# One more pair of head jobs as sums of blocks, leaner head chunks and five attention units at once, in a hybrid mLSTM and windowed-attention step

## The chip, the core and the metric

One core of a Trainium2 chip runs the whole program in one launch. The metric is device microseconds from start to end. Before the change the median of three runs is 858.66 us (856.5 to 862.46).

## The reference

One layer of a hybrid decoder, on a prompt of 1024 tokens and on 8 decoding samples of 4 tokens each (together 1056 columns), model width 1024:

```
h = rmsnorm(x, g) * (1 + scale(c)) + shift(c);  gate(c)          # c: condition vectors
mq, mk, mv, mi, mf, mo, mz, aq, ak, av, az, gm, ga = split(h @ w_in)
# mLSTM branch: 4 heads of 128, chunks of 128 tokens; per chunk
s   = (q k^T) * exp(dmat - m_hat);  num = s v + w_inter * (q C)
dot = sum(s) + w_inter * (q n);     y = num / max(|dot|, exp(-m_hat))
C'  = decay * C + (w_end * k)^T v;  n' = decay * n + sum(w_end * k)
# attention branch: 8 query heads, 2 key heads of 64, window 128, sinks
o = softmax(q k^T, sink) v
x + gate * ((sigmoid(gm) * (y_m @ w_mo) + sigmoid(ga) * (y_a @ w_ao)) @ w_o), then a final rmsnorm
```

Results are y for prompt and samples, the mLSTM states C, n, m, and the kept keys and values.

## The kernel before

Everything is transposed: tiles have channels on the 128 partitions and tokens along the free side. A large product is done in three parts, for accuracy near float32: operands are split into a high and a low part (`split4`, `block_split`: ACT rounds the high part, DVE subtracts), and hi*hi, hi*lo and lo*hi are added up in one PSUM bank.

**Jobs.** A job is one 128-channel slice of `h @ w_in`: `job` loads and splits its weights one or two jobs ahead (`prefetch`, `preload`, in the list `order`) and calls `piece` three times, for 384, 384 and 288 columns. Each piece is 24 products (8 row blocks of h times three parts). `keep` in `head_jobs` moves the result out of PSUM and stores it in the DRAM tiles `mD[h]` (q, k, v of a head).

**Summed pairs.** `block_products` does two jobs at once with a scheme of seven block products in place of eight: the 1024 prompt columns and the 1024 rows of h are cut in halves, and seven sums or differences of blocks (`t1` to `t4` and plain blocks of h, in `OPERANDS`) are multiplied by sums and differences of weight blocks. Each of the seven is 12 products of 512 columns, so a pair has 84. The sample columns go in 16 small products (`Pair.samples`, `smp`) and one more (`smpo`). PSUM banks are carried from product to product, `filled` copies a bank that two products build on. `sum_blocks` forms `t2`, `t3`, `t4` and then `t1` from h read back from DRAM (`hD`, tiles `hb`); `hook` lets pair 0 wait, in the order written out, for `t2` at its product 6 and `t1` at its product 5. `Pair(head_kv, 3)` makes k and v of head 3; 8 pairs of gates, 2 of query gates and 4 of head gates follow.

**Side work.** TensorE's order is written out by the program (`in_order`): the large products come in sequence, and after each group of three `side.tick()` may put in a step of other work. `Side` keeps streams, each with a largest number of live items and a shortest time between beginnings, in a planned time `side.now` that products move on. A step ends in a `yield` of a lag and of the PSUM banks ("b", "o", "a") that its next step needs; steps that need banks come no sooner than `quiet` after the last visit. Streams: "m" gate values and `head(h)`; "a" attention `unit(g, b0)` (16 of them: scores, softmax, transposes `pt`, products `oT`); "x" `ada_gate`, `sum_blocks` and loads; "s" `sample_attention` and `sample_head(h)`. `side.finish` runs what is left of a stream at once; `side.until` lets planned time pass. DVE and ACT get their order from the scheduler of the language in the part after the first stage, and SP issues all transfers in order.

**A head.** `head(h)` goes over its 8 chunks in groups of 3, 3 and 2 (`GROUPS`): `load` fetches q, k, v and two broadcast rows; `stage_a` turns k (`tk`, into `kn`) and v (`tv`, into `vn`) and scales vn by `wend` into `vw`; `stage_a1` and `stage_a2` form the decay matrix `et` with DVE and the exponential; `stage_b` makes `S`, multiplies, and carries the state C on by `U`; `stage_c` to `stage_d` form the result, its norm and its transpose. A group holds seven half tiles: q, k, v, et, qw, kn, vn. All such tiles come from one pool of 43 (`ht`).

**After the pairs** come 16 jobs with `w_ao` and `w_mo`, then the output product `fo` with the residual and the last norm.

Of the kernel before, what the change touches and what calls it, by code (L numbers as in the profile page):

```python
# [10 lines left out]
F32 = mybir.dt.float32  # L11
# [161 lines left out]
def body(tc, a):  # L173
    nc = tc.nc
    with ExitStack() as ctx:
# [76 lines left out]
        side = Side(stores, {"m": (2, 35.0), "a": (4, 9.0), "x": (2, 0.0), "s": (1, 0.0)}, 2.0)  # L252
# [626 lines left out]
        def sample_attention():  # L879
            qpad, vns, kTs = at["qpad"], at["vns"], at["kTs"]  # L880
            kc, vc, kcT = ([ht([128, 4, 128], f"{n}{u}") for u in range(2)] for n in ("kc", "vc", "kcT"))
# [8 lines left out]
            for u in range(2):  # L890
                tq = pb([128, 4, 128], f"kctp{u}")
                for j in range(4):
                    tr(tq[:, j], kc[u][:, j], ident)
                S.copy(kcT[u], tq)
                yield 3.0, "b" if u == 0 else "o"
            sc = po([128, 2, WIN + NS], "scs")
            for u in range(2):
                for w in range(4):
                    b = u * 4 + w
                    qb = qpad[:, b].rearrange("p k g t -> p (k g t)")  # L900
                    r = slice(32 * w, 32 * w + 32)
                    mm(sc[r, u, 0:WIN], qb, kcT[u][:, w], start=True, stop=True)
                    mm(sc[r, u, WIN:], qb, kTs, start=True, stop=True)
# [21 lines left out]
            pT = ht([128, 4, 128], "pTs")  # L925
# [41 lines left out]
        def head_jobs(h):  # L967
            mD[h] = [dp.tile([128, SEQ], F32, name=f"{n}D{h}") for n in "qkv"]
# [28 lines left out]
        mD = {}  # L997

        def head(h):
# [15 lines left out]

            def stage_a(p):
                cs = GROUPS[p]
                m, j0 = len(cs), h * 8 + cs[0]
                w = m * 128
                q, k, v, e_, qw = w_[p]  # L1020
                t129 = lambda t: t[:, :387].rearrange("p (c e) -> p c e", e=129)
                tk = pb([128, 3, 128], f"tk{h}_{p}")
                for i, c in enumerate(cs):
                    tr(tk[:, i], k[:, i * 128:i * 128 + 128], ident)
# [3 lines left out]
                for i, c in enumerate(cs):  # L1028
                    tr(tv[:, i], v[:, i * 128:i * 128 + 128], ident)
# [6 lines left out]
                et, ns = e_[:, :384].rearrange("p (c e) -> p c e", e=128), t129(e_)  # L1036
                w_[p] = q, k, kn, vn, vw, et, qw, ns

            def stage_a1(p):
                m = len(GROUPS[p])  # L1040
                q, et, qw = w_[p][0], w_[p][5], w_[p][6]
                V.tensor_tensor(et[:, :m], et[:, :m], cmask.unsqueeze(1).to_broadcast((128, m, 128)), op=ALU.add)
                V.tensor_tensor(qw[:, :m], qw[:, :m], q[:, :m * 128].rearrange("p (c e) -> p c e", e=128), op=ALU.mult)

            def stage_a2(p):
                j0 = h * 8 + GROUPS[p][0]
                et = w_[p][5]
                for i in range(len(GROUPS[p])):
                    S.activation(et[:, i], et[:, i], AF.Exp, bias=an[:, j0 + i:j0 + i + 1])

            def stage_b(p):
                cs = GROUPS[p]
                m, j0 = len(cs), h * 8 + cs[0]
                q, k, kn, vn, vw, et, qw, ns = w_[p]
                S_ = po([128, 3, 128], f"S{h}_{p}")
                for i, c in enumerate(cs):
                    mm(S_[:, i], k[:, i * 128:i * 128 + 128], q[:, i * 128:i * 128 + 128], start=True, stop=True)
                V.tensor_tensor(et[:, :m], et[:, :m], S_[:, :m], op=ALU.mult)
# [12 lines left out]
                w_[p] = vn, et, qw, chain, ns  # L1071
# [41 lines left out]
            for visit in ([(load, 0), 10.0, "b"], [(stage_a, 0), 3.0, ""], [(stage_a1, 0), 4.0, ""], [(stage_a2, 0), 6.0, "o"],  # L1113
                          [(stage_b, 0), (load, 1), 10.0, "ob"], [(stage_c, 0), (stage_a, 1), 3.0, ""], [(stage_c2, 0), (stage_a1, 1), 4.0, ""],
                          [(stage_a2, 1), 6.0, "o"], [(stage_b, 1), (stage_c3, 0), (load, 2), 4.0, "b"], [(stage_d, 0), 6.0, "ob"],
                          [(stage_c, 1), (stage_a, 2), 3.0, ""], [(stage_c2, 1), (stage_a1, 2), 4.0, ""], [(stage_a2, 2), 6.0, "o"],
                          [(stage_b, 2), (stage_c3, 1), 4.0, "b"], [(stage_d, 1), 6.0, "o"], [(stage_c, 2), 3.0, ""], [(stage_c2, 2), 7.0, ""], [(stage_c3, 2), 5.0, "b"],
                          [(stage_d, 2), 0.0, ""]):
                for fn, p in visit[:-2]:
                    fn(p)  # L1120
                yield visit[-2:]
# [264 lines left out]
        class head_kv:  # L1386
            names = lambda h: (("mk", h), ("mv", h))
            ahead = lambda self, i: None

            def evac(self, c, th, *src):  # L1390
                t = ht([128, 512], "mkv")
                if len(src) == 2:
                    V.tensor_tensor(t, src[0], src[1], op=ALU.add)
                else:
                    S.copy(t, src[0])
                store(mD[self.i][1 + c][:, HALF[th]], t)
                self.held[c, th] = True
                if len(self.held) == 4:
                    side.add("m", head(self.i))

            def samples(self, o):
                for c, t in enumerate((ks, vs)):
                    V.tensor_copy(t[:, self.i], o[:, c])
# [136 lines left out]
        order += [(n, h) for h in range(NH) for n in ("mq", "mk", "mv") if h < NH - 1 or n == "mq"]  # L1540
# [151 lines left out]
        pairs = [Pair(head_kv, NH - 1)] + [Pair(gate, d) for d in range(KT)] + [Pair(query_gate, i) for i in range(2)] + [Pair(head_gate, h) for h in range(NH)]  # L1692

        def hook(n, i):
            if n == 0 and i in (6, 5):
                side.until(lambda: {6: "t2", 5: "t1"}[i] in formed)
            if i == 6:
                if pairs[n].kind is query_gate:
                    side.until(lambda: len(units_done) == 16)
                side.until(lambda: len(samples_done) >= {head_kv: 0, gate: 0, query_gate: 1, head_gate: pairs[n].i + 2}[pairs[n].kind])  # L1700
# [226 lines left out]
```

## Time and profile before

| | before |
|---|---|
| median of 3 runs | 858.66 us |
| profiled execution: time / span of its instructions | 857.83 us / 856.0 us |
| mean granted TensorE clock | 0.995 |
| TensorE busy | 832.8 us |
| DVE busy | 564.8 us |
| ACT busy | 387.6 us |
| GpSimd busy | 30.6 us |
| moved by DMA | 146.48 MB |

Busy time of a matmul is modelled and products overlap, so two of them in a row are better read by their starts. In the rows below, PE is TensorE's products, PEld its weight loads, SPq the queue that issues transfers; "x12" counts instructions; text in brackets or after an arrow names what ended an idle time. A product in plain float32 is two rows in the trace.

### The profile page before, as it was taken

The numbers are of one execution on the slowest core, as the hardware profiler recorded it, in microseconds if no ns is written. First come the engines' busy times: TensorE is split into PE (matmuls) and PEld (weight loads), VectorE is DVE, ScalarE is ACT, GpSimd is POOL, SyncE is SP. The second block draws the span as 40 slices with busy tenths as digits, with TensorE's granted clock in tenths as the row PEclk, the third lists the DMA queues.
The fourth block names the chain that finished last, engine by engine and source line by source line (L and its number), as shares of the span: only waits on it lengthen the run. The fifth ranks groups of instructions, "written<-read, shape, count | busy, mean of one in ns | idle before, by whom it ended". The sixth has DMA issues, their size and how long they took to land.

```text
span 856.0 us, 15320 instructions
## 1 busy us (share of the span) xinstructions
PE 832.8 (97%) x5274; PEld 704.7 (82%) x5274; DVE 564.8 (66%) x1608; ACT 387.6 (45%) x995; POOL 30.6 (4%) x65
## 2 busy tenths in 40 slices
PE   6899999999989999999999999999999999999996
PEld 2689999888869997888888887777778999987785
DVE  4877783534668678565566457687876657747586
ACT  4762355554556555455555444444445332223231
POOL 0000000000000000000000000000001102220000
PEclk9999999999999999999999999999999999999998
DMA  9996448354765657435433323554435788352502
GB/s 327 366 336 211 128 140 284 105 151 147 228 173 162 183 150 227 148 113 168 132 134 103 109 98 116 169 175 124 125 112 177 255 287 309 124 160 104 179 25 80
DMA packets 114609, 146.48 MB, mean 171 GB/s; under 512 B 27120, under 2 KB 71792, under 8 KB 114500
## 3 DMA queue, kind: packets, MB, share of 16 engines
q1 hardware_dynamic: 114532, 145.52, 52.7%
q8 instruction: 41, 0.67, 0.3%
q14 instruction: 36, 0.29, 0.1%
HBM read 107.50 MB, written 38.99 MB: 171 GB/s over the span
## 4 chain that ended last, share of the span: by engine, by line
PE 66%; DVE 2%; DMA 1%; issue 1%; ACT 0%; SPq 0%; DVEq 0%
PE fo L257 11%; PE bx L257 9%; PE by L257 9%; PE bw L257 9%; PE g_w_mo L257 5%; PE g_w_ao L257 5%; PE bz L257 5%; PE g_mq L257 2%; PE smp L257 2%; PE g_mk L257 1%; PE g_mv L257 1%; PE n L257 1%; DMA hb<-hD 1%; PE S L257 1%; PE U L257 1%
## 5 line engine op out<-in xcount | busy, mean ns | idle before, releaser
L257 PE MATMUL g_w_ao<-ya,wh_w_ao 128*128 128x384 f32 (+1 forms) x192 | 45.6, 322 | 0.1
L257 PE MATMUL g_w_mo<-ym_l,wh_w_mo 128*128 128x384 f32 (+1 forms) x192 | 45.7, 323 | 0.0
L219 ACT ACTIVATE p<-p,nmx 128x256 f32<-128x256 f32 (+1 forms) x64 | 31.0, 486 | 20.3 <-DVE nmx L219 16.0
L219 ACT ACTIVATE fjk<-rows_l 128x512 bf16<-128x512 f32 (+2 forms) x19 | 11.6, 609 | 50.8 <-DVE rows_l L219 26.7
L257 PEld LDWEIGHTS g_w_ao<-ya,wh_w_ao 128*128 128x128 f32 x192 | 33.5, 188 | 0.6 <-DVE ya L219 0.4
L257 PEld LDWEIGHTS g_w_mo<-ym_l,wh_w_mo 128*128 128x128 f32 x192 | 33.5, 188 | 0.0
L219 DVE CUSTOM_DVE_ANT_0 p<-sc,cst,sink 128x256 f32<-128x256 f32 (+1 forms) x64 | 26.1, 463 | 11.1 <-PE sc L257 11.1
L257 PE MATMUL g_mq<-h_h,wh_mq 128*128 128x384 f32 (+1 forms) x96 | 32.9, 343 | 0.0
L257 PE MATMUL g_aq<-h_h,wh_aq 128*128 128x384 f32 (+1 forms) x96 | 32.4, 337 | 0.0
L257 PE MATMUL g_aq<-h_l,wh_aq 128*128 128x384 f32 (+1 forms) x96 | 31.0, 323 | 0.0
L257 PE MATMUL g_aq<-h_h,wl_aq 128*128 128x384 f32 (+1 forms) x96 | 31.0, 323 | 0.0
L257 PE MATMUL g_mq<-h_l,wh_mq 128*128 128x384 f32 (+1 forms) x96 | 31.0, 323 | 0.0
L257 PE MATMUL g_w_mo<-ym_l,wl_w_mo 128*128 128x384 f32 (+1 forms) x96 | 31.0, 323 | 0.0
L257 PE MATMUL g_mq<-h_h,wl_mq 128*128 128x384 f32 (+1 forms) x96 | 30.9, 322 | 0.0
L257 PE MATMUL g_w_ao<-ya,wl_w_ao 128*128 128x384 f32 (+1 forms) x96 | 30.8, 321 | 0.0
L257 PE MATMUL g_mv<-h_h,wh_mv 128*128 128x384 f32 (+1 forms) x72 | 24.6, 342 | 0.0
L257 PE MATMUL g_mk<-h_h,wh_mk 128*128 128x384 f32 (+1 forms) x72 | 24.5, 341 | 0.0
L257 PE MATMUL g_mk<-h_h,wl_mk 128*128 128x384 f32 (+1 forms) x72 | 23.2, 323 | 0.0
L257 PE MATMUL g_mv<-h_h,wl_mv 128*128 128x384 f32 (+1 forms) x72 | 23.2, 323 | 0.0
L257 PE MATMUL g_mv<-h_l,wh_mv 128*128 128x384 f32 (+1 forms) x72 | 23.2, 323 | 0.0
L257 PE MATMUL g_mk<-h_l,wh_mk 128*128 128x384 f32 (+1 forms) x72 | 23.2, 323 | 0.0
L219 DVE TENSOR_TENSOR fot<-fo,rows_l 128x512 f32<-128x512 f32 (+1 forms) x17 | 11.2, 657 | 15.3 <-PE fo L257 10.9
(1384 smaller groups left out, 2628.6 us busy)
## 6 DMA issues: line engine op xcount, KB each, us to landing
hb<-hD SPq DMA_DIRECT2D x24, 256.0 KB
x<-xT SPq DMA_DIRECT2D x16, 256.0 KB
early_h<-w_ada SPq DMA_DIRECT2D x8, 512.0 KB
hD<-x SPq DMA_DIRECT2D x16, 256.0 KB
adar_ga<-w_ada SPq DMA_DIRECT2D x16, 256.0 KB
wr_ga<-w SPq DMA_DIRECT2D x16, 256.0 KB
wr_gm<-w SPq DMA_DIRECT2D x16, 256.0 KB
taD<-gt SPq DMA_DIRECT2D x16, 256.0 KB
```

Of the source, the lines that this page charges most:

```text
L219: ins = f(*args, **kw)
L257: in_order(nc.tensor.matmul(out, lhsT, rhs, start=start, stop=stop, skip_group_check=more))
```

## The change

- `inner` lists the 12 head jobs. The first eight stay single jobs. The last four become two summed pairs: v of head 2 with q of head 3, and k with v of head 3. `head_kv` becomes `head_in`, which takes any two jobs and scales q. `head_part` counts the parts of a head and begins `head(h)` when all six are there.
- `sum_blocks` begins, and the units change to the other score bank, at the same distance from the end of the single jobs as before. `ada_gate` has a stream "g" of its own, finished one job before the end.
- A head's group holds five half tiles. k is turned and scaled by `wend` on its way out of PSUM, back into k's own tile; the turned v, with its column of ones, goes into v's own tile and is not scaled. `S` and its product with `et` move from `stage_b` into `stage_a`; `prep` and `stage_e` take the place of `stage_a1` and `stage_a2`, ahead of it. The lags between the steps change.
- Five units may be live, begun 8.0 apart (four and 9.0 before); the quiet time is 1.5 (2.0 before).
- `sample_head(0)` is no longer begun after head 0's jobs, but with the other three after head 3 is done. `sample_attention` uses its key tiles again for the turned keys and for the turned weights.

```diff
-        side = Side(stores, {"m": (2, 35.0), "a": (4, 9.0), "x": (2, 0.0), "s": (1, 0.0)}, 2.0)
+        side = Side(stores, {"m": (2, 35.0), "a": (5,8.0), "x": (2, 0.0), "s": (1, 0.0), "g": (1, 0.0)}, 1.5)
...
-                S.copy(kcT[u], tq)
+                S.copy(kc[u], tq)
...
-            pT = ht([128, 4, 128], "pTs")
+            pT = kc[0]
...
-            if h == NH - 2:
-                side.finish("x")
-                side.add("x", sum_blocks())
-            if h == NH - 1:
-                sc_bank[:] = po, "o+"
-                next(work)
-                job(("mq", h), keep(q, qs, float(128 ** -0.5), "s"), lambda: next(work))
-                return
-            job(("mq", h), keep(q, qs, float(128 ** -0.5), "s"))
-            job(("mk", h), keep(k, ks, 1.0, "s"))
-            job(("mv", h), keep(v, vs, 1.0, "s"))
-            side.add("m", head(h))
+            for n, dst, smp, scale in (("mq", q, qs, float(128 ** -0.5)), ("mk", k, ks, 1.0), ("mv", v, vs, 1.0)):
+                if (n, h) not in order:
+                    return
+                i = order.index((n, h)) - order.index(None)
+                if i == -4:
+                    side.add("x", sum_blocks())
+                if i == -1:
+                    side.finish("g")
+                    sc_bank[:] = po, "o+"
+                    next(work)
+                job((n, h), keep(dst, smp, scale, "s"), (lambda: next(work)) if i == -1 else None)
+                head_part(h, 2)
...
+            def prep(p):
+                V.tensor_tensor(et[:, :m], et[:, :m], cmask..., op=ALU.add)
+                V.tensor_tensor(qw[:, :m], qw[:, :m], q..., op=ALU.mult)
+            def stage_e(p):
+                for i in range(len(GROUPS[p])):
+                    S.activation(et[:, i], et[:, i], AF.Exp, bias=an[:, j0 + i:j0 + i + 1])
             def stage_a(p):
-                kn = ht([128, 3, 128], "kn")
-                S.copy(kn[:, :m], tk[:, :m])
...
-                vn = ht([128, 3, 129], "vn")
+                S_ = po([128, 3, 128], f"S{h}_{p}")
+                for i in range(m):
+                    mm(S_[:, i], blk(k, i), blk(q, i), start=True, stop=True)
+                vn, ns = t129(v), t129(e_)
                 S.copy(vn[:, :m, 0:128], tv[:, :m])
                 G.memset(vn[:, :m, 128:129], 1.0)
-                vw = t129(v)
                 for i in range(m):
-                    S.activation(vw[:, i], vn[:, i], AF.Copy, scale=wend[:, j0 + i:j0 + i + 1])
+                    S.activation(blk(k, i), tk[:, i], AF.Copy, scale=wend[:, j0 + i:j0 + i + 1])
+                V.tensor_tensor(et[:, :m], et[:, :m], S_[:, :m], op=ALU.mult)
...
             def stage_b(p):
-                    mm(Un[:, i], kn[:, i], vw[:, i], start=True, stop=True)
+                    mm(Un[:, i], kn[:, i * 128:i * 128 + 128], vn[:, i], start=True, stop=True)
...
-            if h == NH - 1:
-                for i in range(1, NH):
+            if h == NH-1:
+                for i in range(NH):
                     side.add("s", sample_head(i), "ob")
...
-        class head_kv:
-            names = lambda h: (("mk", h), ("mv", h))
+        class head_in:
+            names = lambda i: paired[i]
             def evac(self, c, th, *src):
+                n, h = self.names[c]
+                scale = float(128 ** -0.5) if n == "mq" else 1.0
                 t = ht([128, 512], "mkv")
                 if len(src) == 2:
                     V.tensor_tensor(t, src[0], src[1], op=ALU.add)
-                else:
-                    S.copy(t, src[0])
+                    src = (t,)
+                if len(src) == 1 and (src[0] is not t or n == "mq"):
+                    S.activation(t, src[0], AF.Copy, scale=scale)
...
-        order += [(n, h) for h in range(NH) for n in ("mq", "mk", "mv") if h < NH - 1 or n == "mq"]
+        inner = [(n, h) for h in range(NH) for n in ("mq", "mk", "mv")]
+        paired = list(zip(inner[8::2], inner[9::2]))
+        order += inner[:8]
...
-        pairs = [Pair(head_kv, NH - 1)] + ...
+        pairs = [Pair(head_in, i) for i in range(len(paired))] + ...
...
-        side.add("x", ada_gate())
+        side.add("g", ada_gate())
...
-            if h == 0:
-                side.add("s", sample_head(0), "ob")
```

More of the change, by code (lines that the diff above doesn't have):

```diff
@@ L967, in head_jobs @@
         def head_jobs(h):
-            mD[h] = [dp.tile([128, SEQ], F32, name=f"{n}D{h}") for n in "qkv"]
             q, k, v = mD[h]
@@ L1045, in stage_a2 @@
[L1045 to L1049, printed above, removed]
+                    S.activation(blk(k, i), tk[:, i], AF.Copy, scale=wend[:, j0 + i:j0 + i + 1])
+                V.tensor_tensor(et[:, :m], et[:, :m], S_[:, :m], op=ALU.mult)
+                w_[p] = k, vn, et, qw, ns
             def stage_b(p):
@@ L1393, in evac @@
                     V.tensor_tensor(t, src[0], src[1], op=ALU.add)
-                else:
-                    S.copy(t, src[0])
[L1396 to L1399, printed above, removed]
-            def samples(self, o):
-                for c, t in enumerate((ks, vs)):
-                    V.tensor_copy(t[:, self.i], o[:, c])
+                    src = (t,)
+                if len(src) == 1 and (src[0] is not t or n == "mq"):
+                    S.activation(t, src[0], AF.Copy, scale=scale)
+                store(mD[h]["mq mk mv".split().index(n)][:, HALF[th]], t)
+                head_part(h, 1)
+            def samples(self, o):
+                for c, (n, h) in enumerate(self.names):
+                    if n == "mq":
+                        V.tensor_scalar(qs[:, h], o[:, c], float(128 ** -0.5), None, op0=ALU.mult)
+                    else:
+                        V.tensor_copy({"mk": ks, "mv": vs}[n][:, h], o[:, c])
         class gate:
@@ L1690, in ada_gate @@
             dma(c32, hD[:, :, SEQ:T])
-        pairs = [Pair(head_kv, NH - 1)] + [Pair(gate, d) for d in range(KT)] + [Pair(query_gate, i) for i in range(2)] + [Pair(head_gate, h) for h in range(NH)]
+        pairs = [Pair(head_in, i) for i in range(len(paired))] + [Pair(gate, d) for d in range(KT)] + [Pair(query_gate, i) for i in range(2)] + [Pair(head_gate, h) for h in range(NH)]
         def hook(n, i):
@@ L1699, in hook @@
                     side.until(lambda: len(units_done) == 16)
-                side.until(lambda: len(samples_done) >= {head_kv: 0, gate: 0, query_gate: 1, head_gate: pairs[n].i + 2}[pairs[n].kind])
+                side.until(lambda: len(samples_done) >= {head_in: 0, gate: 0, query_gate: 1, head_gate: pairs[n].i + 2}[pairs[n].kind])
             if (n, i) in LOADS:
```

56 lines of the change are left out of this document (29 added, 27 removed).

## The prediction

> **What bounds the kernel now.** I read the page's shares first, then its clock line, then TensorE's own idle time by stage.
>
> ```profile
> span 856.0 us, 15320 instructions
> ...
> PE 832.8 (97%) x5274; PEld 704.7 (82%) x5274; DVE 564.8 (66%) x1608; ACT 387.6 (45%) x995; POOL 30.6 (4%) x65
> ...
> PEclk9999999999999999999999999999999999999998
> ```
>
> TensorE is busy 97% of the span at a granted clock that stays at the top. The windows (columns: length, then busy time of PE, weight loads, DVE, ACT and POOL, clock, DMA share, GB/s) show what a gain could be made of:
>
> ```profile
> 85.00:180.00 95.00, 94.10 (x687) 83.87 (x686) 57.84 (x225) 46.58 (x147) 1.06 (x3) 1.00 0.49 156
> 180.00:240.00 60.00, 58.41 (x453) 49.59 (x453) 31.62 (x110) 30.93 (x96) 1.10 (x8) 1.00 0.61 187
> 240.00:300.00 60.00, 59.15 (x442) 54.00 (x441) 42.23 (x146) 34.76 (x109) 1.20 (x7) 1.00 0.64 179
> 300.00:345.00 45.00, 43.52 (x297) 37.53 (x296) 35.70 (x109) 24.87 (x66) 0.48 (x3) 1.00 0.60 184
> 345.00:668.00 323.00, 323.00 (x1914) 260.71 (x1912) 213.49 (x520) 155.26 (x356) 9.38 (x23) 1.00 0.42 133
> ```
>
> From 85 to 345 us, which holds the attention units, the head jobs and the first summed pair, TensorE idles 0.90 + 1.59 + 0.85 + 1.48 = 4.8 us. From 345 to 668 us, the summed pairs, it idles not at all. DVE is busy 0.61, 0.53, 0.70, 0.79 and 0.66 of these five stretches, ACT at most 0.58. So time comes out of this kernel mostly by taking products off TensorE, and goes into it by making TensorE's ordered list wait. The next view names who makes it wait.
>
> ```profile
> PE gp L257 <- ACT adas_ga L219: 1.6, 1, 1.6
> ...
> PE pt L262 <- ACT p L219: 0.9, 1, 0.9
> PE sU L257 <- ACT kn L219: 0.9, 1, 0.9
> PE by L257 <- DVE mkv L219: 0.8, 1, 0.8
> ...
> PE smp L257 <- ACT kn L219: 0.5, 1, 0.5
> ```
>
> These five are 4.7 us, nearly all of the 4.8. `gp` belongs to `ada_gate`, `sU` to `sample_head`, `pt` to an attention unit, `by` and `smp` to the first summed pair.
>
> **The change part by part.** *One more pair of jobs as sums of blocks.* The program's lists say that ("mv", 2) and ("mq", 3) lose 144 products in pieces: 96 of 384 columns and 48 of 288. The new pair brings 84 products of 512 columns, 16 `smp` calls and one `smpo`. Everything else on TensorE keeps its count. The chain of waits, in order of time, prices these:
>
> ```profile
> 353.22 0.17 PE smpo L257 x2
> ...
> 356.22 1.01 PE smp L257 x32
> ...
> 437.95 2.77 PE bw L257 x12
> ...
> 544.82 1.01 PE smp L257 x32
> ...
> 566.61 1.01 PE smp L257 x32
> ...
> 710.22 46.45 PE g_w_mo L257 x288
> ```
>
> The `w_mo` row is eight jobs in the same 2 to 1 mix of 384 and 288 columns, undisturbed: 46.45/288 = 0.1613 us for each product. Removed: 144 x 0.1613 = 23.2 us. Added: 84 x 2.77/12 = 19.4, plus 1.01 (the trace counts 32 for these 16 calls), plus 0.17, together 20.6 us. Net -2.6 us. A check: from `smp` to `smp` one whole pair lasts 566.61 - 544.82 = 21.8 us, 1.2 above my sum, with some visits of the sample heads inside.
>
> *More visits.* Side work (units, heads, sample heads) stands between the large products in visits. Counted in the two orders, the changes from large to small products and back go from 271 to 285: seven visits more, from the shorter quiet time (1.5 for 2.0) and from the two halves of `ada_gate` being split up. What a visit costs beside its own work:
>
> ```profile
> 300.84 0.34 PE L257 MATMUL g_mq<-h_h,wl_mq 128*128 128x384 f32 x1
> 301.02 0.61 PE L257 MATMUL n<-vn,et 128*128 128x129 f32 x4
> ...
> 302.70 0.42 PE L257 MATMUL g_mq<-h_h,wh_mq 128*128 128x384 f32 x1
> 302.96 0.33 PE L257 MATMUL g_mq<-h_l,wh_mq 128*128 128x384 f32 x1
> 303.13 0.34 PE L257 MATMUL g_mq<-h_h,wl_mq 128*128 128x384 f32 x1
> ```
>
> Going in costs nothing (0.18 us to the next start, as inside a job). Coming out, the first product holds the array 0.26 us, the second 0.17: 0.09 us more. Seven visits: +0.6 us.
>
> *`ada_gate` in a stream of its own.* Before, `side.finish("x")` at head 2 ran the rest of `ada_gate` at once, so that `gp` stood directly behind the products whose copy it needs; that is the wait of 1.6 us. After, stream "g" is already empty when `side.finish("g")` comes: 105 products stand between the last `ada_ga` and `gp`. Behind the old wait stood only the products of job ("mq", 2), so nothing else was late by it. -1.6 us.
>
> *Sample head 0 moved* from beside head 1 to behind head 3. Its three `sU` stood where ACT was late with a head's `kn` (0.9 us). The other three sample heads, which already run behind head 3, wait for nothing between 345 and 668 us. -0.9 us. There are now four of them one after the other in the summed pairs; in the emission order the last is done four products ahead of where `head_gate` 3 begins, exactly as before, so no hook waits longer. Its six loads and six stores on SP's queue and its memsets on POOL move with it, from a stretch with a DMA share of 0.64 into one with 0.42. The loads of `sum_blocks` move the other way, two jobs earlier, to a share of 0.61. I take 0 for both.
>
> *Heads with five half tiles.* TensorE's work is the same. On ACT one copy a chunk goes (`kn`), and 32 scalings change their source:
>
> ```profile
> L219 ACT ACTIVATE hv<-vn,wend 128x129 f32<-128x129 f32 x32 | 10.7, 398 | 0.5
> ...
> L219 ACT COPY kn<-tk 128x384 f32<-128x384 f32 (+1 forms) x12 | 5.3, 443 | 2.3 <-PE tk L262 2.3
> ...
> L219 DVE TENSOR_TENSOR et<-et,S 128x384 f32<-128x384 f32 (+1 forms) x12 | 6.1, 506 | 2.6 <-PE S L257 2.5
> ```
>
> That frees 5.3 us of an engine that is at most 0.58 busy: 0 us on the path. In the new order `S`, the three exponentials and the product `et*S` stand in one visit, so DVE can wait in its queue for TensorE and ACT; behind it stand weight splits (`wl_`) and score maxima. The nearest row is its wait for `S`, 2.5 us in 2 waits. At 1.25 us in each of the 12 chunks DVE would lose 15 us; between 180 and 345 us alone it is idle 165 - 109.6 = 55 us. That idle time is the cover; without it the 15 us would stand on the path. I take 0, with 0 and +3 kept as ends. Fewer half tiles held also let loads start earlier: 0 on the path, since no wait of TensorE on a transfer is in its list.
>
> *DVE.* The pair adds 11 instructions there (sums, splits, additions). At the 0.67 us of the row below that is 7 us more, beside TensorE's work, in the stretches with 0.70 and 0.79 load.
>
> *The last block of `t2`.* Pair 0 starts earlier now, and its second product needs `t2`.
>
> ```profile
> 320.67 0.67 DVE L219 TENSOR_TENSOR t2l<-hb,t2h 128x512 fp32r<-128x512 f32 x1
> ...
> 322.55 0.39 PE L257 MATMUL bw<-t2h,wh_phead_kv__3894 128*128 128x512 f32 x1
> 322.78 0.39 PE L257 MATMUL bw<-t2l,wh_phead_kv__3894 128*128 128x512 f32 x1
> ```
>
> DVE ends the last `t2l` at 321.34; TensorE wants it at 322.78: 1.4 us to spare. In the order of before that write stands 10 products ahead of its use, in the new one 5 ahead. Five products of 0.231 are 1.2 us: the spare time is used up. Bounds: below, 0; above, the 2 us that three late DVE instructions take. I take +0.2.
>
> *Sum:* -2.6 + 0.6 - 1.6 - 0.9 + 0.2 = -4.3 us. The profiled execution took 857.83 us (span 856.0 and 1.8 around it), so its like would take 853.5 us. The median of the runs is 858.66, 0.8 above the profiled one, which gives 854.3 us. A change of under 1% (8.6 us) is about what a measurement of this kernel can't tell from none.
>
> **The rivals.** *A: the units make TensorE wait (slower than before).* Five units at once, begun 8.0 apart for 9.0, still share two score banks and two transpose banks. Where ACT and DVE finish a softmax late, the ordered list stops at `pt`, between 85 and 230 us. The price of one such wait is the 0.9 us of the row `pt <- ACT p`; one of 16 units pays it now. From six units on (5 x 0.9 = 4.5 us more) it eats the gain of 4.3; with all 16 it is +13.5 us, so 854.3 + 13.5 = 867.8 us; with ten paying, 862.4. For it: units overlap more. Against it: ACT and DVE have 40% of that stretch idle, and the lags between a unit's steps (2.5, 3.0, 7.0, 5.0) stay.
>
> *B: the pair does not give what it says.* The first summed pair had two of the five waits (`by` 0.8, `smp` 0.5); with a second pair of head jobs while heads still load DVE, two pairs pay them, and at the 21.8 us of the check row the pair costs 1.2 us more than I summed: 854.3 + 1.3 + 1.2 = 856.8 us. For it: 0.79 DVE load there. Against it: the units now end before the pair begins.
>
> *C: much faster.* All idle time of 85 to 345 us goes, visits cost nothing: -2.6 - 4.8 = -7.4, 851.3 us. No row of idle time carries more, so faster by over 1%, under 850.1 us, needs something else.
>
> *D: a product of 512 columns costs no more than one of the old mix* (0.161 us, were there a fixed price for each product): 84 x 0.161 + 1.2 = 14.7 us for the pair, a net of -8.5 instead of -2.6, so 848.4 us. Against it stands the `bw` row, 0.231 us each, while the mean of the old mix, 352 columns, has 0.161: the price goes with the columns.
>
> The Trainium skill, "TensorE: Matmul & The Clock Gate", section "Back-to-back issue gap", gives about 131 ns for each product of 512 columns in a sustained stream, which as an estimate would make the pair 84 x 0.131 + 1.2 = 12.2 us. The trace does not agree with its 0.231, and that decides.
>
> **How the numbers follow.** My forecast, between 852 and 856: 0.50. B, and mixtures of it with a late `t2`, 856 to 859: 0.20. C and what lies beneath it, 0.11; D 0.01. A with some units, 859 to 863: 0.10; A with nearly all, and other waits of that size: 0.08. The range is 849 to 862.5 us and leaves about 0.15 out. Faster by over 1% is D and the lower part of C, 0.08; slower by over 1% (867.2) is a part of A, 0.07; the rest, 0.85, lies within 1%.
>
> **What would show it.** In the profile after, the `g_mv` rows should have a third fewer products, the `g_mq` rows a quarter fewer, at the same mean, and the `smpo` rows two more. The list of TensorE's waits should have lost `gp` and `sU`; a wait of `bw` for DVE's `t2l` may be new. The windows from 85 us on should still show TensorE full, with the end of the head jobs some 24 us earlier and one more pair behind them. Heads should have no `kn` copy and `et*S` soon behind `S`. Wrong would be: several waits of `pt` or `oT` on ACT or DVE (A), summed pairs 23 us apart with idle time in them (B), or starts of products of 512 columns more than 0.235 us apart.

## The result, and the profile after

The changed kernel takes 855.05 us (median, 853.87 to 857.44) against 858.75 us (856.32 to 862.46) of the kernel before in the same comparison: a ratio of 0.9959, with a 95% interval of 0.9949 to 0.9969. That is 3.7 us, small but outside the noise, since the interval stays below 1; the forecast was 4.3 us, to 854.3. The profiled execution took 854.31 us, where the sum had made 853.5.

The page of the kernel after, its first lines and the clock:

```profile
span 852.5 us, 15278 instructions
...
PE 829.6 (97%) x5248; PEld 697.5 (82%) x5248; DVE 569.5 (67%) x1619; ACT 386.7 (45%) x987; POOL 30.9 (4%) x63
...
PEclk9999999999999999999999999999999999999998
```

TensorE is still the bound, at the same granted clock, with 26 products fewer. The groups by shape show the products that went (count behind the x, then busy time and mean ns of one):

```profile
L257 PE MATMUL g_mk<-h_h,wh_mk 128*128 128x384 f32 x48 | 17.4, 362 | 0.0
L257 PE MATMUL g_mq<-h_h,wh_mq 128*128 128x384 f32 x48 | 17.3, 361 | 0.0
...
L257 PE MATMUL g_mv<-h_h,wh_mv 128*128 128x384 f32 x32 | 11.6, 362 | 0.0
```

`g_mv` has 32 where `g_mk`, which was not changed, has 48: a third fewer. `g_mq` has 48 where the kernel before had 64: a quarter fewer. The means are within 6 ns of those before (356 to 358 ns). The chain of waits after, at its end, shows where the time did not change:

```profile
664.46 42.09 PE g_w_ao L257 x263
706.55 46.45 PE g_w_mo L257 x288
753.00 91.65 PE fo L257 x440
```

From `w_mo` to the end all lasts as long as before (within 0.2 us), and `g_w_mo` begins 3.67 us earlier (706.55 for 710.22 of the prediction's row). So the whole gain lies ahead of it. TensorE's list of waits after, without those of the first 30 us, which both kernels have:

```profile
PE pt L262 <- ACT p L219: 1.5, 2, 0.8
PE ada_ga L257 <- ACT p L219: 1.3, 1, 1.3
...
PE bx L257 <- ACT gt L219: 1.2, 1, 1.2
```

The waits of `gp`, `sU`, `by` and `smp` (3.8 us) are gone, two others have come and `pt` waits twice instead of once: 4.0 us in all, where there were 4.7. No `bw` waits for `t2l`. By stretches:

```profile
85.00:180.00 95.00, 94.19 (x692) 82.93 (x690) 61.35 (x245) 48.21 (x156) 0.85 (x2) 1.00 0.52 163
180.00:240.00 60.00, 58.68 (x469) 50.73 (x468) 34.34 (x115) 34.99 (x111) 1.25 (x4) 1.00 0.67 202
240.00:300.00 60.00, 59.28 (x439) 53.10 (x438) 42.22 (x145) 33.28 (x96) 1.26 (x7) 1.00 0.61 178
300.00:345.00 45.00, 45.00 (x282) 37.18 (x281) 29.95 (x77) 23.93 (x59) 0.21 (x2) 1.00 0.52 177
345.00:668.00 323.00, 321.70 (x1909) 257.88 (x1908) 220.04 (x547) 151.00 (x345) 10.09 (x27) 1.00 0.44 131
```

The stretch from 300 to 345 us, which lost 1.48 us before, now loses nothing. The first summed pair has moved into the stretch ahead of it (its first `bx` starts at 285.4 us, before at 314.7), and that one loses 0.72 us, where it lost 0.85 without the pair. Not all got better: the summed pairs from 345 to 668 us, where TensorE idled not at all, now lose 1.30 us, 1.2 of them at the wait of `bx`.

### The profile page after: what moved, and what is told of

Same layout as the page of the kernel before. It is cut to its first block, busy times and chain, and to the rows that moved or that the text cites. A ratio compares the mean times of both kernels' runs of the same rounds, so it can differ in the third digit from the quotient of the medians.

```text
span 852.5 us, 15278 instructions
## 1 busy us (share of the span) xinstructions
PE 829.6 (97%) x5248; PEld 697.5 (82%) x5248; DVE 569.5 (67%) x1619; ACT 386.7 (45%) x987; POOL 30.9 (4%) x63
## 4 chain that ended last, share of the span: by engine, by line
PE 93%; DVE 3%; ACT 2%; DMA 1%; issue 1%; SPq 0%; DVEq 0%
PE fo L257 11%; PE bx L257 11%; PE by L257 10%; PE bw L257 10%; PE g_aq L257 6%; PE g_w_mo L257 5%; PE bz L257 5%; PE g_w_ao L257 5%; PE g_mq L257 4%; PE g_mk L257 3%; PE g_mv L257 3%; PE sc L257 2%; PE smp L257 2%; PE oT L257 2%; PE g_ak L257 2%; PE pt L262 1%
## 5 line engine op out<-in xcount | busy, mean ns | idle before, releaser
L219 DVE CUSTOM_DVE_ANT_0 p<-sc,cst,sink 128x256 f32<-128x256 f32 (+1 forms) x64 | 26.1, 464 | 11.9 <-PE sc L257 10.0
L257 PE MATMUL g_mq<-h_h,wh_mq 128*128 128x384 f32 (+1 forms) x72 | 24.8, 344 | 0.0
L257 PE MATMUL g_mq<-h_h,wl_mq 128*128 128x384 f32 (+1 forms) x72 | 23.2, 323 | 0.0
L257 PE MATMUL g_mq<-h_l,wh_mq 128*128 128x384 f32 (+1 forms) x72 | 23.2, 322 | 0.0
L219 DVE SCALAR_TENSOR_TENSOR u_h<-tgw_ao,g_w_ao 128x384 f32<-128x384 f32 (+1 forms) x24 | 12.3, 518 | 11.8 <-PE g_w_ao L257 11.5
L219 DVE SCALAR_TENSOR_TENSOR tgw_mo<-tgw_mo,g_w_mo 128x384 f32<-128x384 f32 (+1 forms) x24 | 12.5, 519 | 10.3 <-PE g_w_mo L257 10.3
L257 PEld LDWEIGHTS g_aq<-h_h,wh_aq 128*128 128x128 f32 x96 | 18.0, 188 | 1.4 <-issue 1.0
```

The costliest lines, as they stand in the source:

```text
L219: ins = f(*args, **kw)
L257: in_order(nc.tensor.matmul(out, lhsT, rhs, start=start, stop=stop, skip_group_check=more))
```

## The experiments

All twelve kernels are the one before or the one after with one thing undone, added or moved, or with several (e2, e6, e10). The ratio is to the kernel before as measured beside each, whose median lay between 858.58 and 859.88 us. The starts of the profiled executions differ, so the table also has the profiled span from the first `sc` (the first attention unit) on, the sum of TensorE's waits from 85 us on, and the time from 85 to 840 us in which the granted clock was 0.50; the last section comes back to that column. For the kernel after, the first `sc` is in this row:

```profile
L257 PE MATMUL sc<-ukv,uqv x128: 272/376/481, 95.1 to 245.6; 64*128 64x256 f32 x112, 64*128 64x128 f32 x16
```

With the span of 852.5 us that makes 852.5 - 95.1 = 757.4 us. The others are worked out in the same way.

| kernel | median us | ratio to before, 95% | from the first `sc` us | waits us | at clock 0.50 us |
|---|---|---|---|---|---|
| before | 858.75 | | 761.4 | 4.7 | 0 |
| after | 855.05 | 0.9949 to 0.9969 | 757.4 | 4.0 | 0 |
| e1_one_pair | 861.31 | 1.0019 to 1.0043 | 763.2 | 6.7 | 0 |
| e2_pair_units | 864.86 | 1.0045 to 1.0077 | 768.0 | 9.0 | 6.8 |
| e3_heads7 | 866.71 | 1.0079 to 1.0114 | 768.2 | 11.9 | 6.8 |
| e4_three_pairs | 882.05 | 1.0253 to 1.0279 | 782.0 | 26.8 | 20.5 |
| e5_sample0_early | 864.64 | 1.0057 to 1.0094 | 765.7 | 8.6 | 3.4 |
| e6_heads7_s0 | 873.09 | 1.0144 to 1.0188 | 775.8 | 16.8 | 13.7 |
| e7_gate_in_x | 866.85 | 1.0074 to 1.0120 | 769.3 | 9.1 | 6.8 |
| e8_heads_alone | 860.32 | 0.9997 to 1.0035 | 764.2 | 5.2 | 6.8 |
| e9_stores_act | 860.17 | 0.9994 to 1.0030 | 757.1 | 3.7 | 0 |
| e10_sample0_early_stores_act | 868.14 | 1.0068 to 1.0120 | 763.2 | 6.7 | 3.4 |
| e11_gap_82 | 858.55 | 0.9966 to 1.0002 | 757.1 | 3.3 | 0 |
| e12_units_4_9 | 865.31 | 1.0035 to 1.0077 | 764.9 | 8.0 | 3.4 |

### The pair: one, two and three

e1 is the kernel after with one summed pair, as before:

```diff
-        paired = list(zip(inner[8::2], inner[9::2]))
-        order += inner[:8]
+        paired = list(zip(inner[10::2], inner[11::2]))
+        order += inner[:10]
```

> The new kernel with only one summed pair (k and v of head 3), ten single jobs; heads, units and streams as in the new one. Theory (TensorE's list of products sets the time): the pair's gain of 2.6 us is gone, visits go from 142 to 139 (-0.3 us), so 855.05 + 2.3 = 857.4 us, ratio to before 0.998. Rival (the gain comes from the leaner heads and the units, the pair is paid for by later waits): it keeps the gain, 854.5 to 855.5 us, ratio 0.996.

Measured: 861.31 us. Without the second pair, the rest of the change is 2.6 us slower than the kernel before. Both theories missed. The products that come back are 2.6 us, and 2.7 us of new waits (6.7 for 4.0) come with them; together 5.3 of the 5.8 us by which it is longer from the first `sc` on.

e4 goes the other way, with three pairs (`inner[6::2]`, `inner[7::2]`, `inner[:6]`).

> The new kernel with one more pair: the jobs from q of head 2 on are three summed pairs. Theory: -2.6 us once more, one visit more, unless the blocks t2 are late, for which TensorE waits up to 2 us: 852.4 us (852 to 855), ratio to before 0.993. Rival (each further pair starts the blocks while the units still hold half tiles, and TensorE waits): 855 us or more, ratio 0.996 or more.

Measured: 882.05 us. The products are 2.6 us fewer, and two waits of nearly 10 us each swallow that more than seven times over. The rival holds. TensorE's list of waits, and the second of the two in the timeline (start, length, instruction, in brackets the idle time ahead of it and what ended it):

```profile
PE tv L262 <- ACT yt L219: 9.8, 1, 9.8
PE gp L257 <- ACT adas_ga L219: 9.6, 1, 9.6
```

```profile
285.04 0.69 DVE L219 TENSOR_TENSOR hb<-hb,hb 128x512 f32<-128x512 f32 x1 [2.54 <-DMA hb<-hD]
...
290.06 0.69 DVE L219 TENSOR_TENSOR hb<-hb,hb 128x512 f32<-128x512 f32 x1 [2.95 <-DMA hb<-hD]
290.83 0.58 ACT L219 ACTIVATE yt<-ty,vec 128x384 f32<-128x384 f32 x1 [4.45 <-DVE hb L219]
291.31 0.61 ACT L219 CAST h_h<-hb 128x512 fp32r<-128x512 f32 x1
291.46 0.90 PE L262 MATMUL tv<-cst,hv 128*128 128x128 f32 x3 [9.78 <-ACT yt L219]
```

Read it from the top. VectorE adds blocks of h and waits twice for their loads. ScalarE's next step is the copy of `ty` (a head's result) into `yt`; the rounding of the added block comes behind it, at 291.31. The copy reads nothing of `hb`, and still it starts only when VectorE's addition is done. What the two share is the pool of 43 half tiles, so `yt` most likely waits for a half tile that the addition sets free; no row names the tile. `tv` follows as soon as `yt` has left the PSUM bank of `ty`, so TensorE waits 9.8 us. None of TensorE's rows names a load, and yet the chain goes back to a load. The first wait, of `gp`, is the one that the prediction wanted gone: here `side.finish("g")` comes before the gate's stream is empty.

### The units' limits

e12 is the kernel after with the units of before:

```diff
-  "a": (5,8.0),
+  "a": (4, 9.0),
```

> The kernel after with one part undone: four attention units at once and 9.0 planned us apart, as before, with the pair, the new heads and the shorter quiet time kept. Visits are as many as in after. Theory A (the prediction's price of 0 for the units): 855.0 us within 1 us. Theory B (the units now end after the first summed pair has begun, so that VectorE and ScalarE carry both, as with three pairs, where that cost 27 us): 860 to 868 us with waits of pt and tv between 240 and 330 us.

Measured: 865.31 us. Theory B holds in size, and in place for the longest wait, of `by` at 317 us; no `tv` waits, and the wait of `bx` stands at 620 us, far behind the units. The last `sc` starts at 265.6 us (245.6 in after), while the first summed pair starts in both at 285 us, so the tails of the units reach into it: their last product `oT` starts at 290.6 us, in after at 274.3. Its waits, and the stretch behind the longest of them:

```profile
PE by L257 <- DVE mkv L219: 2.2, 1, 2.2
...
PE bx L257 <- ACT hg L219: 1.7, 1, 1.7
...
PE pt L262 <- ACT p L219: 1.1, 1, 1.1
PE pt L262 <- ACT hk L219: 1.0, 2, 0.7
```

```profile
314.00:318.00 4.00, 1.85 (x6) 1.17 (x5) 3.04 (x6) 2.58 (x6) 0.00 (x0) 0.85 0.17 62
318.00:322.00 4.00, 4.00 (x15) 3.18 (x14) 1.26 (x2) 1.36 (x4) 0.00 (x0) 0.72 0.96 300
```

The wait of 2.2 us has a second price: the granted clock (third number from the end) is 0.85 and 0.72 in the two slices, so the products of the second slice run at 72% of the full clock on average. That is 1.1 us on top.

### The heads

e8 is the kernel before with the new heads alone. e3 is the kernel after with the heads of before, this diff read backwards (the lags between the steps, not shown, change with it):

```diff
-  kn = ht([128, 3, 128], "kn"); S.copy(kn[:, :m], tk[:, :m])
-  S.activation(vw[:, i], vn[:, i], AF.Copy, scale=wend[...])
+  S.activation(blk(k, i), tk[:, i], AF.Copy, scale=wend[...])
...
+  S_ = po(...)    # and its products: from stage_b into stage_a
```

> The kernel before with the new heads alone (five half tiles a chunk, products S in the first stage), everything else as it was: one summed pair less, four units. Theory (the prediction's 0 us for the heads): 858.7 within 1 us. Rival (each part alone upsets the hand-set order and the gain is in their sum, as the units with the pair and the old heads took 6 us more): 861 to 865 us with new waits at pt, tv or by. A gain of over 1 us would say that the shorter heads save TensorE time by themselves, most likely the waits of by and smp in the first summed pair (1.3 us).

> The new kernel with the heads of before (seven half tiles a group, S in stage_b, the old lags). Theory: TensorE's work is the same and the heads are off the path; visits 138 for 142 (-0.4 us): 854.2 to 855.6 us, ratio to before 0.995 to 0.996. Rival (five half tiles are what frees the loads and gives 1 to 2 us): 856 to 857 us, ratio 0.997 to 0.998.

Measured: 860.32 us and 866.71 us. By themselves the new heads gain nothing, and the interval of the first leaves open whether they lose anything; inside the whole, their absence costs some 12 us, where both theories had at most 857 us. The list of waits of e3 and the stretch behind its longest wait:

```profile
PE sty L262 <- DVE sns L219: 5.5, 1, 5.5
PE pt L262 <- ACT p L219: 3.9, 3, 2.4
```

```profile
651.00:657.00 6.00, 0.51 (x4) 0.25 (x3) 5.25 (x21) 1.15 (x5) 0.57 (x1) 0.71 0.77 162
657.00:662.00 5.00, 5.00 (x17) 4.00 (x18) 0.25 (x1) 0.53 (x2) 0.00 (x0) 0.66 1.05 282
```

`sty` belongs to a sample head. With the older, longer chain of visits the heads end later in the order, the four sample heads behind them are not done when `head_gate` 3 wants the last of them, its remaining steps stand one behind the other, and TensorE runs dry (0.51 us busy in six). The prediction's "the last is done four products ahead" does not hold with the heads of before. Most of the cost lies in this late part: of the 10.8 us by which e3 is longer from the first `sc` on, only 1.4 lie ahead of the first gate pair (237.5 us for 236.1), and 9.4 between it and the first `g_w_ao` (338.1 for 328.7).

e6 was to test that: the heads of before, and sample head 0 again behind head 0, so that only three are left.

```diff
+            if h == 0:
+                side.add("s", sample_head(0), "ob")
...
-                for i in range(NH):
+                for i in range(1, NH):
```

> The kernel after with the heads of before (seven half tiles a chunk), which took 866.7 us, and beside that sample head 0 behind head 0 again, so that only three sample heads are left for the summed pairs. Theory (the heads cost little by themselves; their later end left too little time for the fourth sample head, so that TensorE stood 5.5 us at sty and lost clock behind it): the sty wait is gone or under 1 us and the time falls by 5 to 7 us to 860 to 862. Rival (the heads of before cost the time themselves, through pt and tk waits while the units run): 865 to 867 us with the sty wait gone and pt waits of 4 us left.

Measured: 873.09 us. The `sty` wait is gone, as expected, but the time went up by some 6 us. Other waits took its place where the heads, the last units and the first pair overlap:

```profile
PE g_mk L257 <- ACT mk L219: 4.8, 1, 4.8
PE pt L262 <- ACT p L219: 4.1, 2, 3.3
PE tv L262 <- ACT smps L219: 4.1, 1, 4.1
```

So both theories fell: with the heads of before, sample head 0 costs more early than late, and its late place is not the whole cost of those heads.

e2 has the second pair and the units' new limits on the kernel before, with the old heads, and the gate in its old stream:

```diff
-  side = Side(stores, {..., "a": (4, 9.0), ...}, 2.0)
+  side = Side(stores, {..., "a": (5, 8.0), ...}, 1.5)
...
+  paired = list(zip(inner[8::2], inner[9::2]))
+  order += inner[:8]
```

> The kernel of before with the second summed pair and the new limits of the streams (five units, 8.0 apart, quiet time 1.5) alone: heads with seven half tiles, ada_gate in stream x and finished at head 1's second job, sample head 0 early. Theory: products -2.6 us, seven visits more +0.6, the wait of gp stays, some of the waits of the first pair stay: 858.75 - 2.0 = 856.7 us, ratio 0.9977. Rival (without the leaner heads the pool of 43 half tiles runs out and loads come late): TensorE waits for transfers, slower than before, 859 to 865 us.

Measured: 864.86 us. The theory missed by 8 us. The rival's size fits, but its mechanism is not shown: no wait in TensorE's list from 85 us on names a transfer, and VectorE's waits on loads of `et` between 180 and 400 us, 12.4 us, are no longer than in before (12.2), which is 6 us shorter. After has 2.1.

### Sample head 0 and the gate's stream

e5 is the kernel after with the diff of e6 alone (and the new heads). e7 is the kernel after with the gate in the old stream:

```diff
                 if i == -4:
+                    side.finish("x")
                     side.add("x", sum_blocks())
                 if i == -1:
-                    side.finish("g")
...
-        side.add("g", ada_gate())
+        side.add("x", ada_gate())
```

> The kernel after with one part undone: sample head 0 stands behind head 0 again, among the heads, and not behind head 3. Theory (the prediction's own step, worth 0.9 us, and visits at 0.09 us each): side work is entered six times less often in this order, -0.5 us, and three sU stand again where ScalarE can be late, +0.9 us: 855.4 us, with a wait of sU for ScalarE in TensorE's list and no sty wait. First rival (the move gave nothing of its own, since TensorE is only as late as the whole mixture of side work makes it): within 0.5 us of 855.0, and other waits in the list of about the same sum. Second rival (sample head 0 loads ScalarE and VectorE just where the units end, as the waits of 2 us did with one part alone): 858 to 861 us, with pt or tv among the waits.

> The kernel after with the ada_gate work put back into the stream of the units' own follow-up work, where it is finished at one blow when the gate is wanted. Theory (the prediction's step, -1.6 us for the wait of gp): gp stands behind the copy that it needs again, +1.6 us, and the new wait of ada_ga for ScalarE's p (1.3 us) goes: 855.4 us if both are as sized, 856.6 if only the first is. Rival (waits on ScalarE are set by its load and only change their place): 855.0 within 0.5 us and a sum of waits of 4 us as now.

Measured: 864.64 and 866.85 us, where the prediction had priced these two steps at 0.9 and 1.6 us. Undoing either costs more than 9 us against the kernel after, more than any theory or rival had. The wait that returns in e7 at `gp` is only 0.7 us; the others in its list are new:

```profile
PE bx L257 <- DVE zt L219: 2.5, 1, 2.5
...
PE S L257 <- ACT et L219: 2.1, 1, 2.1
PE tv L262 <- ACT smps L219: 1.3, 1, 1.3
```

In e5 the longest wait is of `S`, 3.2 us. The timelines of ScalarE and of SyncE's queue show where it begins, and the timeline of all engines how it goes on:

```profile
284.83 0.70 ACT L219 ACTIVATE et<-et,an 128x128 f32<-128x128 f32 x2 [3.37 <-DVE et L219]
285.44 0.47 ACT L219 ACTIVATE mk<-g_mk 128x384 f32<-128x384 f32 x1
```

```profile
280.75 0.38 SPq L245 DMA_DIRECT2D qw<-wid  x1
285.93 0.32 SPq L245 DMA_DIRECT2D kD<-mk  x1
...
287.78 0.39 SPq L245 DMA_DIRECT2D et<-nmd  x1
```

```profile
292.90 0.56 DVE L219 TENSOR_TENSOR et<-et,cst 128x384 f32<-128x384 f32 x1 [3.12 <-DMA et<-nmd]
...
293.50 0.40 ACT L219 ACTIVATE et<-et,an 128x128 f32<-128x128 f32 x1 [2.89 <-DVE et L219]
...
296.73 0.47 ACT L219 COPY et<-n 128x387 f32<-128x387 f32 x1
...
297.25 1.01 PE L257 MATMUL S<-hq,hk 128*128 128x128 f32 x3 [3.22 <-ACT et L219]
```

SyncE issues nothing for 5 us, since the next in its queue is a store (`kD<-mk`) of what ScalarE copies out only at 285.44: ScalarE itself had stood still for 3.37 us behind VectorE's step on an earlier `et`. The load of the next `et`, behind the store, goes out at 287.78, and VectorE gets it at 292.90. ScalarE's exponentials wait for VectorE; the copy of `n`, behind them, comes at 296.73; and `S` starts as soon as that copy has emptied the bank of `n`.

### Are late loads the cause?

e9 and e10 test this chain. They are the kernel after and e5 with the delayed stores issued from ScalarE's queue, so that no load stands behind them:

```diff
-                    issue(*e[1:])
+                    issue(*e[1:], eng=S)
...
-        def issue(out, in_, late=False):
-            ins = nc.sync.dma_start(out, in_)
+        def issue(out, in_, late=False, eng=None):
+            ins = (eng or nc.sync).dma_start(out, in_)
+            if eng is not None:
+                return
```

> The kernel after with one thing changed that the emission order does not see: the delayed stores of the jobs' and units' results are issued from ScalarE's queue and not from SyncE's, where the loads of the heads and of the summed pairs stand behind them. Between 180 and 400 us SyncE waits some 85 us in these stores for the copies of ScalarE. Theory (loads that come late by this hold up VectorE, behind it ScalarE, and TensorE last): VectorE's waits on loads between 180 and 400 us, 13 us now, fall below 6, and of TensorE's 4.0 us of waits up to half go: 853 to 855 us. Rival (the waits come from the order and the load of ScalarE alone, which now issues a hundred transfers more): 856 to 862 us with longer waits of pt.

> The kernel after with sample head 0 behind head 0 again, which took 864.6 us, and beside that the delayed stores issued from ScalarE's queue. Its emission order of TensorE, VectorE and ScalarE's computing is that of the run of 864.6 us. Theory (late loads behind waiting stores make the waits): VectorE's wait of 13.1 us for the et loads falls below 5, TensorE's 3.2 us at S goes, and the time falls to 855 to 858 us. Rival (the order itself makes TensorE wait, whatever the loads do): 862 to 867 us with S, pt and tv in the list of waits as they are now.

Measured: 860.17 and 868.14 us, both longer than with the stores on SyncE. e9 lies in its rival's range, e10 above both of its ranges. The test is less clean than the expectations say: in the traces TensorE's order is the same, product for product, but the scheduler has laid VectorE's and ScalarE's work anew (against after, some 190 of VectorE's 1619 instructions and some 80 of ScalarE's 987 stand elsewhere in e9). A wait ahead of all the units is new in both, of `gp` at 67 us for ScalarE (4.4 us in e9), the granted clock is 0.50 from 68.5 to 78.8 us in e9, and the first `sc` starts at 103 us, not at 95 or 96. From the first `sc` on, though, e9 is 0.3 us shorter than after and e10 2.5 us shorter than e5. The rows of e10 for TensorE and for VectorE:

```profile
PE pt L264 <- ACT p L219: 4.2, 4, 2.2
...
PE S L259 <- DVE C L219: 0.5, 1, 0.5
```

```profile
DVE et L219 <- DMA et<-nmd: 6.0, 4, 1.8
```

VectorE's wait for `et` fell from 13.1 to 6.0 us and the wait of `S` from 3.2 to 0.5: that fits the chain read from the timelines, though the new order of the two engines may have a part in it. But of the 8.3 us by which e5 is longer than after from the first `sc` on, 6.1 us (763.2 for 757.1) are left with the stores out of the way. `pt` now waits 4.2 us. Of the 6.1 us, 3.0 are other waits (6.7 for 3.7) and 1.7 the half clock behind the longest of them (3.4 us at 0.50); the rest is not accounted for. So late loads are one cause and not the main one here: moving sample head 0 costs 6.1 of its 8.3 us even without them.

### Is every other order worse?

Of the kernels so far, none with another order had come near the one after, so it was possible that any shift in the order costs this much. e11 changes a number that no step speaks of: units begin 8.2 apart and not 8.0.

> The kernel after with one number changed that no step of the prediction speaks of: attention units begin at least 8.2 planned us apart, not 8.0. No work is added or taken away, and five units still run at once; from TensorE's first thousand products on, side work falls between other products. Theory A (the gain belongs to the parts that were changed): 855.0 us within 1 us, with waits from 85 us on of 4 us in sum as now. Theory B (the neighbours ran 5 to 27 us longer because any new order lets TensorE meet other results late, and the order of after has few such places): 858 to 865 us with 5 to 10 us of waits, other ones than now.

Measured: 858.55 us, 0.9984 of the kernel before (0.9966 to 1.0002). By its time it lies in theory B's range. The profiled execution tells more: its first `sc` starts at 98.9 us, 3.8 later than in after, though TensorE's order is the same up to 233 us and the other two engines' up to 227. The clock is what differs there: from 10 to 37 us it is 0.75 on average, in after 0.94. From the first `sc` on it takes 757.1 us, 0.3 less than after, and its waits are 3.3 us, where theory B had 5 to 10:

```profile
PE bx L257 <- DVE zt L219: 2.5, 1, 2.5
...
PE pt L262 <- ACT p L219: 0.8, 1, 0.8
```

So in this execution theory B falls for the stretch in which the order differs: other waits, nearly the same sum, the same time. One other order is a small sample, and it differs only behind 233 us. In the orders that cost more, several of the waits lie where units, heads, sample heads and the first pair meet; that this meeting is the reason is argued, not shown. Whether the whole of e11's longer median lies in the start is not settled by one profiled execution.

## Why the prediction was right, point by point

The forecast was 0.6 us from the measured change, but in part by luck: one step was too large by 1.8 us, and another 1.0 us came from where no step had looked.

- **Products, -2.6 us: right.** From the starts of TensorE's products between 66 us and the first `g_w_ao`, the pieces of 384 and 288 columns lose 23.1 us and the 84 products of 512 columns with their `smp` and `smpo` bring 20.4: -2.6 us. Rival D (a product of 512 columns at 0.161 us) is out: `bw` rows of 12 products still last 2.77 us. The first summed pair starts 29 us earlier, where the prediction had some 24.
- **Seven more visits, +0.6 us: right.** The same starts show 126 visits before and 133 after, and 0.6 us more of time around them, as seven changes from small to large products at 0.09 us each would cost.
- **`gp` and `sU`, -2.5 us: the step that was mis-sized.** Both waits went, and `by` and `smp` with them, 3.8 us. But `ada_ga` now waits 1.3 us: in a stream of its own it is let in behind a unit's transposes while ScalarE still works on that unit's `p`. And `bx` waits 1.2 us, `pt` 0.6 us more. The sum of the waits fell by 0.7 us, not 2.5. Another 1.0 us came from small products in new company, which no step had priced: measured from start to start, `S` and `U` (64 products each) take 1.6 us less, the sample work 0.8 and `gp` 0.5, while `tv`, `pt` and `os` take 1.6 more. It is by luck that this put the sum nearly right: -2.6 + 0.6 - 0.7 - 1.0 = -3.7.
- **`t2l`, +0.2 us: 0.** It is in no list of waits.
- **Heads and units at 0 us: right for the whole, wrong as prices.** Inside the change they are needed: without the units' limits the kernel is 7.5 us longer, without the new heads 10.8, both from the first `sc` on. Of the 7.5 us, 4.2 lie ahead of the first gate pair; of the 10.8, only 1.4. The prediction said it for the units ("the units now end before the pair begins") but as an argument against rival B, with no price for the case that they did not. It named VectorE's idle time as the cover of the heads; it did not name what e3 lost most by, that the four sample heads must still fit behind them. That this is the whole worth of the new heads is not shown, since e6, with only three behind them, was longer still.
- **Loads at 0 us: the reason was wrong.** "No wait of TensorE on a transfer is in its list" does not exclude it: the timelines of e4 and e5 show a late load that reaches TensorE as a wait on ScalarE. What the new kernel gains there is small: between 180 and 400 us VectorE's waits on loads are 13.3 us in all in after and 16.9 in before, of which the loads of `et` have 2.1 and 12.2.
- **The rivals.** B is excluded, and C was not reached, since new waits replaced the old. A was given 0.18. Its mechanism (a softmax that comes late at `pt`) is only one among those of the slower kernels, but its size was common: the twelve neighbours of this change ran 858.6 to 882.1 us, where A had 859 to 868. The forecast held because this version has an order with few waits. The profile of before could not show that, only that 4.7 us of waits were to be had at most; in this too the forecast had luck.

Shown are the prices of products and visits, the chain from a load in e5 (that of e4 up to the half tile), and that the parts need each other. Not shown is why each of the other waits stands where it does.

## What to carry to other kernels

Price the products of a change from undisturbed rows; that part of a sum can be trusted to a few tenths. Do not price the parts of a hand-laid order one by one: where three streams meet on the same two side engines, each part is worth what it keeps clear for the others, and a part undone cost here seven times and more the wait that it was priced at. Before blaming an engine for a wait, follow its idle time back one engine at a time, to the queue of the loads; and run a change without meaning beside the undone parts, to know what a shifted order costs by itself.

## What the runs showed of the hardware

A wait of TensorE can have a price beyond its length, which no step had counted. Behind its waits of 1.8 us (`gp`) and 2.5 us (`tv`), e8 has 3.4 us each at a granted clock of 0.50. The windows around the first:

```profile
238.86:242.27 3.41, 1.65 (x9) 0.56 (x5) 1.32 (x9) 2.44 (x10) 0.00 (x0) 1.00 0.28 52
242.27:245.69 3.42, 3.42 (x22) 2.22 (x21) 1.76 (x7) 1.19 (x4) 0.00 (x0) 0.50 0.08 21
```

At 0.50 the same work takes twice as long, so 3.4 us lose 1.7: in e3, at 658 us, products of 512 columns start 0.43 us apart, not 0.23. With 2.6 us of products and 1.2 us of more waits, the 3.4 us that e8 loses in this way make 7.2, for the 6.8 us by which it is longer than after from the first `sc` on.

The length of the wait does not decide alone, for in e11 the clock stayed at 1.00 behind a wait of 2.5 us:

```profile
565.40:568.81 3.41, 2.12 (x10) 1.39 (x8) 3.30 (x8) 2.00 (x5) 0.00 (x0) 1.00 0.45 156
568.81:572.22 3.41, 2.18 (x9) 1.80 (x10) 3.32 (x6) 0.71 (x2) 0.00 (x0) 1.00 0.05 19
```

The traces show what goes with it. In each, the stretches at 0.50 begin whole multiples of 3.413 us apart (in e8 331.02 - 242.27 = 88.75 us, 26 of them), as if the clock were set anew on a fixed grid. Cut into windows on that grid, the 14 traces have 20 windows between 85 and 840 us in which TensorE idles 1.76 us or more; the window behind each is at 0.50. Where it idles 1.74 us or less, the next is at 1.00, with one exception (e2, 0.9 us idle from 234.7 us on). The wait in e11 falls on an edge of the grid and leaves 1.3 and 1.2 us in two windows; the longest idle time in a window is 1.6 us in before and 1.3 in after. So the same wait can cost 1.7 us more or nothing, by where it falls.

The Trainium skill, "TensorE: Matmul & The Clock Gate", section "Why this matters for your kernels", says to leave no idle gaps of over some 3 us between bursts of products, lest the clock fall back. The direction agrees; the length does not, as 1.8 us were enough here.
